# A hybrid decoder block on one core: the first norm without GpSimd, gates as the first columns, and block sums kept in PSUM for the convolutions

## The chip, the cores and the metric

One NeuronCore of a Trainium2 chip runs the whole program. The metric is device time in microseconds, the median of three runs of the program; beside it stands one execution that the hardware profiler recorded. PE is TensorE (matrix products and transposes), DVE VectorE, ACT ScalarE, POOL GpSimd, SP the engine that issues all DMAs from one queue.

## The reference, cut to what matters

`x` is 1024 tokens by 1024 channels, all float32.

```python
def rmsnorm(x, g):
    return x * lax.rsqrt(jnp.mean(x * x, -1, keepdims=True) + EPS) * g

h = rmsnorm(x, norm_mix)
proj = h @ w_in                      # 1024 x 1024 x 11808
z, xBC, dt_raw, qkv, gate_logits = jnp.split(proj, offs, axis=-1)
y_ssm = mamba2_branch(z, xBC, dt_raw, ...) @ w_ssm_out
    # xBC = silu(causal_depthwise_conv(xBC, conv_w, conv_b)), 4 taps
    # chunked state space scan over 128 tokens, times silu(z), group norm
q, k, v = rope(q), rope(k), v        # 12 heads of 128, three dilated windows
y_att = dilated_attention_branch(q, k, v) @ w_att_out
gates = sigmoid(gate_logits + b_gate)            # 2 x 1024 channels
x = x + (gates[0] * y_ssm + gates[1] * y_att) @ w_mix_out
h = rmsnorm(x, norm_ffn)
x = x + (silu(h @ w_ffn_gate) * (h @ w_ffn_up)) @ w_ffn_down
return rmsnorm(x, norm_final)
```

## The kernel before

**Numbers.** A float32 product is three passes of PE: every operand is split into a rounded high part and the rest (`hhi`, `hlo`; for weights a CAST on ACT and a subtraction on DVE or POOL), and `mm3` adds hi by hi, lo by hi and hi by lo in PSUM. `hhi` and `hlo` hold the normed tokens turned round: channel on the partitions, `[128, token half, depth tile k of 8, 512 tokens]`.

**Columns.** The input projection is 92 columns of 128 channels (and 32 channels of dt): 16 z, 16 x, 4 b, 4 c, 36 for q, k and v, 16 gates. An x, b or c column goes through `conv_silu` (an ACT pass with the bias, three DVE multiply-adds of 1023, 1022 and 1021 elements, one more DVE pass), a z column through an ACT Tanh and two DVE half passes, a gate column through one Tanh on ACT.

**Stages of the projection**, in order: (1) the *head*: the first norm, and two *first columns* that are computed by quarters of 256 tokens, as soon as two of the eight token tiles are ready (`first_quarter`); (2) the *bridge*: `N_BRIDGE` direct columns (48 products of 512 columns each), while the sums for the next stage are made; the dt columns; (3) the *flat* stage: 20 pairs of columns, each by block multiplication with seven products of 12 matmuls instead of eight (class `Seven`): products come in the order 1, 6, 5, 7, 2, 3, 4, each in one of four PSUM tiles `bank` of 512; `prep` makes the weights' sums on POOL and their parts on ACT and DVE; `chain` adds the products up on DVE; `T1` to `T4` are sums of token blocks (POOL first, then DVE). A *heavy* pair is two x columns, or a b and a c; a *light* one two z or two gates; they alternate; (4) the *direct* stage: q, k, v and the remaining gates as direct columns, with the scan and the attention beside them. Merge, FFN (Seven again) and the last norm follow.

**The head.** For each pair `q` of token tiles `stat_task` takes squares on ACT, multiplies the tiles by `norm_mix` (held as `nm`, one row copied to all partitions) on POOL, and finds the inverse root `rs` on DVE with 15 small operations of 128x2 (`rsqrt_steps`); `tile_task` scales the tile by `rs`, and `split_tokens` transposes it on PE into two banks, casts to `hhi` on ACT and subtracts to `hlo` on DVE.

**Order.** A planner (`Pace`) writes the program: tasks are generators that yield the buffers that they need, engines have costs in a small table, and the main line of PE calls `tick` or `due` between matmuls so that ready tasks write their instructions. Order on an engine is fixed by that; at run time only semaphores decide. Buffers come from stores: 31 slots `slab` of 1024, 6 slots `own`, two PSUM tiles `wide` of 1024, four `bank`; a slot is free again when its last reader is done. All records have one line, that of a helper.

## Time and profile before

| what | value |
|---|---|
| median of 3 runs | 2230.18 us (2226.22 to 2230.81) |
| the profiled execution | 2226.1 us, of it 2224.3 us span |
| PE busy, and its mean granted clock | 2154.4 us (97 %), 0.987 |
| DVE, ACT, POOL busy | 1545.7, 879.5, 690.9 us |
| DMA | 299.83 MB, 134 GB/s to and from HBM |

PE works nearly all of the span, so time can be read as PE's work plus the stretches in which it waits (69.9 us) or runs at a lower clock. The span is from the first to the last instruction.

### The profile page before, as it was taken

How to read it: one execution, taken by the hardware profiler on the slowest of the kernel's cores; microseconds unless marked ns; L12 is line 12 of the kernel's file. 1: busy time of each engine (PE TensorE's matmuls, PEld its weight loads, DVE VectorE, ACT ScalarE, POOL GpSimd, SP SyncE). 2: the span in 40 equal slices, each digit the busy share in tenths (PEclk: the TensorE clock that was granted, in tenths of full speed). 3: DMA queues.
4: the chain of work that ended last, by engine and by line, in shares of the span. 5: the costliest groups of instructions: out<-in, count | busy, mean ns of one | idle time of the engine just before them, and what ended most of it. 6: DMA issues, size and time to landing. Idle time of an engine off the chain costs nothing. (4 is left out here: it accounts for less than half of the span.)

```text
span 2224.3 us, 27832 instructions
## 1 busy us (share of the span) xinstructions
PE 2154.4 (97%) x10476; PEld 1781.7 (80%) x10476; DVE 1545.7 (69%) x2094; ACT 879.5 (40%) x1565; POOL 690.9 (31%) x420
## 2 busy tenths in 40 slices
PE   5999999999999999999999999999999999999996
PEld 4777888887888888888888887888778888888885
DVE  7979888876567776765434337644797777757787
ACT  3334444434554555454332224323333233324444
POOL 5233333321344444542103003002445444420102
PEclk8999999999999999999999999999999999999998
DMA  3433434336354555652128457463233333339332
GB/s 126 126 90 108 124 101 124 104 114 202 122 187 123 162 154 160 185 150 73 39 76 248 140 176 245 133 188 123 59 95 109 114 100 96 122 137 346 118 95 100
DMA packets 302587, 299.83 MB, mean 135 GB/s; under 512 B 20028, under 2 KB 246260, under 8 KB 302196
## 3 DMA queue, kind: packets, MB, share of 16 engines
q1 hardware_dynamic: 302452, 298.05, 42.9%
q8 instruction: 82, 1.34, 0.3%
q14 instruction: 53, 0.43, 0.1%
HBM read 225.00 MB, written 73.01 MB: 134 GB/s over the span
## 5 line engine op out<-in xcount | busy, mean ns | idle before, releaser
L165 POOL TENSOR_TENSOR xr<-xr,nfin 128x512 f32<-128x512 f32 x16 | 21.8, 1367 | 185.4 <-ACT jk L165 185.0
L165 POOL TENSOR_TENSOR slab__13_12098<-h2hi,h2lo 128x1024 f32<-128x1024 f32 x1 | 3.1, 3142 | 120.8 <-PE wide__35_11738 L165 120.8
L165 POOL TENSOR_TENSOR slab__11_10598<-slab__11_10598,last__2_10581 128x1024 f32<-128x1024 f32 x1 | 2.5, 2501 | 122.1 <-DMA slab__11_10598<-yt_d 122.1
L165 POOL TENSOR_TENSOR more__3_12094<-h2hi,h2lo 128x512 f32<-128x512 f32 x2 | 2.6, 1294 | 63.2 <-DVE h2lo L165 63.2
L165 POOL TENSOR_TENSOR slab__15_4124<-slab__15_4124,slab__14_4121 128x1024 f32<-128x1024 f32 x1 | 2.3, 2339 | 63.2 <-DVE wide__3_4015 L165 63.2
L165 ACT ACTIVATE jk<-xr 128x512 f32<-128x512 f32 x16 | 10.1, 632 | 16.4 <-DVE xr L165 12.7
L165 POOL TENSOR_TENSOR slab__21_7103<-slab__21_7103,slab__32_9422 128x1024 f32<-128x1024 f32 x1 | 2.4, 2388 | 43.1 <-DMA slab__32_9422<-fd 43.1
L165 POOL TENSOR_TENSOR slab__3_1145<-slab__3_1086 128x512 f32<-128x512 f32 x1 | 1.6, 1554 | 43.3 <-PE bank__6_1094 L165 43.3
L165 PE MATMUL bank__1_281<-ident,slab__1_151 128*128 128x128 f32 x4 | 1.1, 435 | 12.7 <-ACT slab__1_151 L165 12.7
L165 DVE TENSOR_TENSOR rs<-rs,rt 128x2 f32<-128x2 f32 (+2 forms) x30 | 12.4, 412 | 0.8
L165 PE MATMUL wide__4_4172<-hhi,slab__17_3976 128*128 128x512 f32 x16 | 7.9, 495 | 4.6 <-DVE slab__3_4170 L165 4.6
L165 POOL TENSOR_TENSOR slab__48_15496<-slab__23_15188,slab__80_15309 128x512 f32<-128x512 f32 x1 | 1.3, 1292 | 32.1 <-DVE slab__80_15309 L165 32.1
L165 PEld LDWEIGHTS bank__1_281<-ident,slab__1_151 128*128 128x128 f32 x4 | 0.7, 217 | 12.9 <-ACT slab__1_151 L165 12.9
L165 PE MATMUL wide__1_183<-hlo,slab__1_242 128*128 128x256 f32 x32 | 9.6, 299 | 1.1 <-DVE hlo L165 1.1
L165 POOL TENSOR_TENSOR slab__22_9025<-slab__22_9025,slab__14_4121 128x1024 f32<-128x1024 f32 x1 | 2.4, 2404 | 25.8 <-ACT slab__22_9025 L165 25.8
L165 PE MATMUL bank__3_479<-ident,slab__1_154 128*128 128x128 f32 x4 | 1.1, 428 | 9.5 <-DVE slab__1_154 L165 9.5
L165 DVE TENSOR_TENSOR rt<-rt,rv 128x2 f32<-128x2 f32 (+2 forms) x30 | 9.7, 324 | 0.7
L165 PE MATMUL wide__1_183<-hhi,slab__1_242 128*128 128x256 f32 x32 | 9.5, 295 | 0.7 <-ACT hhi L165 0.7
L165 ACT ACTIVATE xr<-xr,or 128x512 f32<-128x512 f32 x8 | 5.8, 719 | 10.6 <-DVE or L165 10.5
L165 DVE TENSOR_TENSOR slab__14_8742<-slab__14_8742,slab__33_9452 128x1024 f32<-128x1024 f32 x1 | 1.2, 1226 | 12.4 <-DMA slab__33_9452<-fd 12.4
L165 DVE TENSOR_SCALAR rv<-sq 128x2 f32<-128x2 f32 x4 | 2.4, 608 | 10.6 <-ACT slab__1_161 L165 10.6
L165 POOL TENSOR_TENSOR slab__10_8743<-slab__10_8743,slab__14_4121 128x1024 f32<-128x1024 f32 x1 | 2.4, 2406 | 22.7 <-ACT slab__10_8743 L165 22.7
(7605 smaller groups left out, 8377.5 us busy)
## 6 DMA issues: line engine op xcount, KB each, us to landing
xr<-x_d SPq DMA_DIRECT2D x8, 512.0 KB, 6.5
out<-xr SPq DMA_DIRECT2D x16, 256.0 KB, 2.1
b_d<-hhi SPq DMA_DIRECT2D x1, 1024.0 KB
b_d<-hlo SPq DMA_DIRECT2D x1, 1024.0 KB, 7.8
slab__1_150<-in_x SPq DMA_DIRECT2D x1, 512.0 KB
slab__1_151<-in_x SPq DMA_DIRECT2D x1, 512.0 KB, 5.1
slab__1_158<-in_norm_mix SPq DMA_DIRECT2D x1, 512.0 KB
slab__1_165<-in_w_in SPq DMA_DIRECT2D x1, 512.0 KB, 7.4
```

Of the source, the lines that this page charges most:

```text
L165: r = call(*args, **kw)
```

## The change

1. **First norm.** POOL no longer multiplies by `norm_mix`. Token tiles 0 to 3 are scaled by `rs` and `nm` in one DVE operation. Tiles 4 to 7 (`half_task`) are only scaled by their `rs`, transposed by depth tile `k` (four tiles into one bank), and `norm_mix`, now a column of `par` after the transposition, is applied as the scale of the copies out of PSUM: `hhi` (ACT), `hlo` (DVE), and a third copy on ACT that is T3 or T2 itself, so that `t_rest` has nothing left to add. The first columns' second token half follows by `k` (`first_half`, 512 tokens wide).
2. **Inverse root.** 12 small operations instead of 15; one root for tiles 4 to 7.
3. **Columns.** Gates 0 and 1 are the first columns instead of b and c of group 0; the bridge is gates 2 to 4 instead of four z; the flat stage has 12 heavy and 8 light pairs instead of 11 and 9, so heavy ones stand next to each other at four places; 11 gates instead of 10 are direct columns.
4. **Flat sums.** The last additions of a pair are written to two `wide` PSUM tiles (for the last pair to `own`), and convolutions, z and gates read them there.
5. **dt.** The chain of dt waits until flat pair 6 and yields between its operations.
6. **From flat to direct.** Before, the first k and the first q column both had their first token half done ahead of the reload of `hhi` and `hlo` (event `b12`); now only k, and q follows whole.
7. `mm3` calls `pace.wait`, which changes the planner's clock and no instruction.

```diff
-N_BRIDGE = 4
-N_FLAT_GATES = 6
+N_BRIDGE = 3
+N_FLAT_GATES = 0
...
         for _ in range(3):
-            nc.vector.tensor_tensor(t, r, r, ALU.mult)
+            nc.vector.scalar_tensor_tensor(t, r, -0.5, r, ALU.mult, ALU.mult)
             yield [t]
             nc.vector.tensor_tensor(t, t, v, ALU.mult)
             yield [t]
-            nc.vector.tensor_scalar(t, t, -0.5, 1.5, ALU.mult, ALU.add)
-            yield [t]
-            nc.vector.tensor_tensor(r, r, t, ALU.mult)
+            nc.vector.scalar_tensor_tensor(r, t, 1.5, r, ALU.add, ALU.mult)
...
+            o = yield from outs()
+            yield from arrive(7, (o["22"], c12), (c21, c21))
             for p, c, name in ((2, c11, "11"), (3, c12, "12"), (4, c21, "21")):
-                yield from arrive(p, (c, c))
+                yield from arrive(p, (o[name], c))
...
-    first = [plan_a(XBC0 + DI)[0], plan_a(XBC0 + DI + 512)[0]]
+    first = [plan_a(GATE0 + i * P)[0] for i in range(2)]
...
-    bridge = [direct("z", 0, f) for f in range(N_BRIDGE)]
+    bridge = [direct("gate", 2 + i) for i in range(N_BRIDGE)]
...
     def stat_task(q):
...
-            if q or i:
-                yield [nm]
-                nc.gpsimd.tensor_tensor(xt.v, xt.v, nm.v, ALU.mult)
...
     def tile_task(i):
...
+        nc.vector.scalar_tensor_tensor(xt.v, xt.v, rs, nm.v, ALU.mult, ALU.mult)
         yield [xt]
-        if i == 0:
-            nc.vector.scalar_tensor_tensor(xt.v, xt.v, rs, nm.v, ALU.mult, ALU.mult)
-        elif i == 1:
-            nc.scalar.activation(xt.v, xt.v, AF.Copy, scale=rs)
-        else:
-            nc.vector.tensor_scalar(xt.v, xt.v, rs, None, ALU.mult)
...
+    def half_task():
+
+        yield "rs2"
+        for i in range(4):
+            xt, rs = xts[4 + i].v, rscale[2][:, i:i + 1]
+            if i % 2:
+                nc.vector.tensor_scalar(xt, xt, rs, None, ALU.mult)
+            else:
+                nc.scalar.activation(xt, xt, AF.Copy, scale=rs)
...
+        for k in range(KD):
+            yield from bank.room()
+            pt = bank.get([P, 512])
+            for i in range(4):
+                tp(pt.v[:, i * P:(i + 1) * P], xts[4 + i].v[:, k * P:(k + 1) * P], ident)
+            hv = hhi[:, 1, k, :]
+            yield [pt]
+            nc.scalar.activation(hv, pt.v, AF.Copy, scale=nm_t(k))
+            nc.vector.scalar_tensor_tensor(hlo[:, 1, k, :], pt.v, nm_t(k), hv.bitcast(F32), ALU.mult, ALU.subtract)
+            nc.scalar.activation(A.T[("T3", "T2")[k // 4]][k % 4 // 2].v[:, k % 2, :], pt.v, AF.Copy, scale=nm_t(k))
+            pt.free()
+            pace.fire(f"hk{k}")
...
+    def first_half():
+        ws = [w_get(first[u]) for u in range(2)]
+        for k in range(KD):
+            pace.until(f"hk{k}")
+            for u, (hi, lo) in enumerate(ws):
+                mm3(fps[u].v[:, 512:], hi[:, k, :], lo[:, k, :], hhi[:, 1, k, :], hlo[:, 1, k, :], k == 0, k == KD - 1)
+                tick()
...
+        def outs():
+            place = own if i == len(flat) - 1 else wide
+            yield from place.room(2)
+            res.extend(place.get([P, S]) for _ in range(2))
...
     for i in range(len(flat)):
+        if i == 6:
+            pace.fire("spare")
...
-    ps = [u(ths=(0,)) for u in units[:2]]
+    ps = units[0](ths=(0,))
     pace.until("b12")
-    for u, t in zip(units[:2], ps):
-        u(t, (1,))
-    units = units[2:]
+    units.pop(0)(ps, (1,))
```

POOL in the head, before, from its first work on; `slab__1_150` to `157` are the token tiles, `158` is `nm`, `165` and `242` the first weight tile and its high part, `670` to `675` the sums for T1 and T4 of token half 0.

```order
L165 TENSOR_TENSOR slab__1_151<-slab__1_151,slab__1_158 128x1024
L165 TENSOR_TENSOR slab__1_243<-slab__1_165,slab__1_242 128x1024
L165 TENSOR_TENSOR slab__1_152<-slab__1_152,slab__1_158 128x1024
L165 TENSOR_TENSOR slab__1_153<-slab__1_153,slab__1_158 128x1024
L165 TENSOR_TENSOR slab__1_154<-slab__1_154,slab__1_158 128x1024
L165 TENSOR_TENSOR slab__1_155<-slab__1_155,slab__1_158 128x1024
L165 TENSOR_TENSOR slab__1_156<-slab__1_156,slab__1_158 128x1024
L165 TENSOR_TENSOR slab__1_157<-slab__1_157,slab__1_158 128x1024
L165 TENSOR_TENSOR slab__1_670<-hhi,hlo 128x1024
L165 TENSOR_TENSOR slab__1_671<-hhi,hlo 128x1024
L165 TENSOR_TENSOR slab__1_674<-hhi,hlo 128x1024
L165 TENSOR_TENSOR slab__1_675<-hhi,hlo 128x1024
```

POOL in the head now, again from its first work on; the last rows are the first flat pair's weight sums.

```order
L166 TENSOR_TENSOR slab__1_596<-hhi,hlo 128x1024
L166 TENSOR_TENSOR slab__1_597<-hhi,hlo 128x1024
L166 TENSOR_TENSOR slab__1_600<-hhi,hlo 128x1024
L166 TENSOR_TENSOR slab__1_601<-hhi,hlo 128x1024
L166 TENSOR_TENSOR slab__2_620<-slab__2_618 128x512
```

The four sums are now POOL's first work; they wait for the two `hlo` operations of token tile 3 and for nothing later.

ACT in the head before, in the second token half: one CAST for each of the banks into which tiles 4 to 7 are transposed.

```order
L165 CAST hhi<-bank__3_479 128x4x128
L165 CAST hhi<-bank__3_486 128x4x128
L165 CAST hhi<-bank__4_491 128x4x128
L165 CAST hhi<-bank__4_501 128x4x128
L165 CAST hhi<-bank__4_547 128x4x128
```

ACT in the head now, where the second token half is scaled and copied out (tiles 4 and 6 are `slab__1_154` and `156`, the banks one depth tile each, `slab__1_447` a part of T3).

```order
L166 ACTIVATE slab__1_154<-slab__1_154,rs_11_269 128x1024
L166 ACTIVATE slab__1_156<-slab__1_156,rs_11_269 128x1024
L166 ACTIVATE hhi<-bank__3_459,par 128x512
L166 ACTIVATE slab__1_447<-bank__3_459,par 128x512
L166 ACTIVATE hhi<-bank__3_467,par 128x512
L166 ACTIVATE slab__1_447<-bank__3_467,par 128x512
L166 ACTIVATE hhi<-bank__4_475,par 128x512
```

Now each bank has two copies on ACT with the `hlo` operation of DVE between them: the second copy waits for that operation, and the bank is free after it.

DVE in the flat stage before, the middle of one heavy pair (`own__2_1063` and `1064` are the pair's two columns, `own__3_1248` and `1268` what `conv_silu` accumulates, banks are products).

```order
L165 TENSOR_TENSOR own__2_1064<-bank__11_1222,own__2_1064 128x512
L165 SCALAR_TENSOR_TENSOR own__3_1248<-own__2_1063,par,own__3_1248 128x1023
L165 SCALAR_TENSOR_TENSOR own__3_1248<-own__2_1063,par,own__3_1248 128x1022
L165 SCALAR_TENSOR_TENSOR own__3_1248<-own__2_1063,par,own__3_1248 128x1021
L165 TENSOR_TENSOR slab__3_1231<-slab__4_1217,slab__3_1231 128x512
L165 SCALAR_TENSOR_TENSOR own__3_1268<-own__2_1064,par,own__3_1268 128x1023
```

DVE in the flat stage now, the same place of a heavy pair that follows another one.

```order
L166 TENSOR_TENSOR wide__6_1443<-bank__12_1447,own__3_1339 128x512
L166 TENSOR_TENSOR wide__6_1444<-bank__12_1468,own__4_1340 128x512
L166 SCALAR_TENSOR_TENSOR own__4_1494<-wide__6_1443,par,own__4_1494 128x1023
L166 SCALAR_TENSOR_TENSOR own__4_1494<-wide__6_1443,par,own__4_1494 128x1022
L166 SCALAR_TENSOR_TENSOR own__4_1494<-wide__6_1443,par,own__4_1494 128x1021
L166 SCALAR_TENSOR_TENSOR own__5_1499<-wide__6_1444,par,own__5_1499 128x1023
L166 SCALAR_TENSOR_TENSOR own__5_1499<-wide__6_1444,par,own__5_1499 128x1022
```

The sum and its reader have moved from `own` (SBUF) to `wide` (PSUM); the next pair's seventh product, the first that is written to a `wide` tile, waits until these readers are done.

SP at the end of the flat stage, before (`in_rope` is the table for q and k, `xq_d` the store of a finished x column).

```order
L165 DMA xq_d_120<-own__17_4034 512x1x256
L165 DMA xq_d_120<-own__13_4045 512x1x256
L165 DMA slab__20_4117<-in_w_in 128x8x128
L165 DMA slab__16_4119<-in_rope 128x1024
L165 DMA slab__14_4121<-in_rope 128x1024
```

SP at the end of the flat stage now (`zq_d` is the store of a finished z column).

```order
L166 DMA zq_d_124<-own__16_3943 512x1x256
L166 DMA zq_d_124<-own__17_3960 512x1x256
L166 DMA slab__17_4008<-in_w_in 128x8x128
L166 DMA slab__3_4010<-in_rope 128x1024
L166 DMA slab__3_4012<-in_rope 128x1024
```

The table's loads stand behind the last pair's stores as before, but the last pair is now a light one.

## Rows read from the trace of the kernel before

**Rows 1.** The page's head and part 1 (engine, busy us, share, instructions).

```profile
span 2224.3 us, 27832 instructions
...
PE 2154.4 (97%) x10476; PEld 1781.7 (80%) x10476; DVE 1545.7 (69%) x2094; ACT 879.5 (40%) x1565; POOL 690.9 (31%) x420
```

**Rows 2.** Waits of PE: us in total, times, longest.

```profile
PE bank__1_281 L165 <- ACT slab__1_151 L165: 12.7, 1, 12.7
PE bank__3_479 L165 <- DVE slab__1_154 L165: 9.5, 1, 9.5
PE wide__4_4172 L165 <- DVE slab__3_4170 L165: 4.6, 1, 4.6
```

**Rows 3.** Timeline of the head, POOL: start us, us, operation, [idle before <-releaser].

```profile
40.80 2.39 POOL L165 TENSOR_TENSOR slab__1_670<-hhi,hlo 128x1024 f32<-128x1024 f32 x1
```

**Rows 4.** Timeline of the head, DVE, at the same time.

```profile
38.54 2.32 DVE L165 TENSOR_TENSOR rt<-rt,rv 128x2 f32<-128x2 f32 x1
...
40.90 2.32 DVE L165 TENSOR_SCALAR rt<-rt 128x2 f32<-128x2 f32 x1
```

**Rows 5.** Timeline of the head, DVE, early.

```profile
8.21 0.17 DVE L165 TENSOR_SCALAR rt<-rv 128x2 int32<-128x2 int32 x1
...
20.80 1.28 DVE L165 SCALAR_TENSOR_TENSOR slab__1_150<-slab__1_150,rs,slab__1_158 128x1024 f32<-128x1024 f32 x1
```

**Rows 6.** Timeline of the head, ACT.

```profile
6.82 1.06 ACT L165 ACTIVATE slab__1_161<-slab__1_151 128x1024 f32<-128x1024 f32 x1
...
20.86 1.15 ACT L165 ACTIVATE slab__1_151<-slab__1_151,rs 128x1024 f32<-128x1024 f32 x1 [5.40 <-DVE rt L165]
23.22 0.59 ACT L165 CAST hhi<-bank__1_281 128x512 fp32r<-128x512 f32 x1 [1.21 <-PE bank__1_281 L165]
...
74.36 1.21 ACT L165 ACTIVATE own__1_662<-wide__1_184,par 128x1024 f32<-128x1024 f32 x1 [1.67 <-PE wide__1_184 L165]
```

**Rows 7.** Windows of the flat stage: us, engines' busy us (instructions), PEclk, DMA.

```profile
130.00:150.00 20.00, 17.84 (x77) 13.89 (x75) 19.36 (x19) 12.17 (x19) 8.18 (x4) 1.00 0.25 72
150.00:190.00 40.00, 35.39 (x138) 28.00 (x139) 36.70 (x43) 15.21 (x24) 19.39 (x10) 0.91 0.33 96
190.00:250.00 60.00, 60.00 (x267) 49.69 (x266) 55.63 (x65) 24.70 (x37) 23.34 (x15) 1.00 0.33 97
```

**Rows 8.** Windows of the passage to the direct stage, columns as before.

```profile
547.50:552.10 4.60, 0.01 (x1) 0.05 (x1) 2.56 (x4) 3.06 (x3) 4.49 (x2) 0.83 1.03 407
552.10:560.00 7.90, 7.90 (x27) 6.25 (x27) 3.96 (x5) 3.54 (x10) 2.14 (x2) 0.67 0.95 294
```

**Rows 9.** Timeline there, SP (time to issue) and DVE.

```profile
538.19 0.51 SPq L165 DMA_DIRECT2D xq_d<-own__13_4045  x1
...
539.49 1.33 SPq L165 DMA_DIRECT2D slab__16_4119<-in_rope  x1
...
546.31 1.23 DVE L165 TENSOR_TENSOR wide__3_4015<-wide__3_4015,slab__16_4119 128x1024 f32<-128x1024 f32 x1 [8.15 <-DMA slab__16_4119<-in_rope]
```

**Rows 10.** Timeline of the head, PE.

```profile
22.06 1.12 PE L165 MATMUL bank__1_281<-ident,slab__1_151 128*128 128x128 f32 x4 [12.70 <-ACT slab__1_151 L165]
```

**Rows 11.** Timeline of the first heavy flat pair, DVE.

```profile
155.43 0.68 DVE L165 TENSOR_TENSOR own__2_1064<-bank__11_1222,own__2_1064 128x512 f32<-128x512 f32 x1
156.03 6.18 DVE L165 SCALAR_TENSOR_TENSOR own__3_1248<-own__2_1063,par,own__3_1248 128x1023 f32<-128x1023 f32 x3
...
162.74 3.91 DVE L165 SCALAR_TENSOR_TENSOR own__3_1268<-own__2_1064,par,own__3_1268 128x1023 f32<-128x1023 f32 x3
...
173.73 2.28 DVE L165 SCALAR_TENSOR_TENSOR own__3_1268<-own__2_1064,own__3_1268 128x1024 f32<-128x1024 f32 x1
```

**Rows 12.** Timeline, DVE with a PSUM operand, and POOL.

```profile
80.69 3.91 DVE L165 SCALAR_TENSOR_TENSOR own__1_662<-wide__1_184,par,own__1_662 128x1023 f32<-128x1023 f32 x3
...
86.01 1.21 DVE L165 SCALAR_TENSOR_TENSOR own__1_629<-wide__1_183,own__1_629 128x1024 f32<-128x1024 f32 x1
...
85.08 2.17 POOL L165 TENSOR_TENSOR slab__2_697<-slab__2_697,slab__2_693 128x512 f32<-128x512 f32 x1
```

More of the change, by code (lines that the diff above doesn't have):

```diff
@@ L297, in due, with wait @@
             self._step(min(ready, key=lambda k: (k[1], k[0], k[2])))
+    def wait(self, out, ins):
+        while True:
+            at = max([self.wr.get(_key(a), (0.0, ""))[0] for a in ins] + [self.rd.get(_key(out), (0.0, ""))[0]])
+            if at <= self.t:
+                return
+            nxt = max(self.t, min([at] + [k[0] for k in self.tasks]))
+            self.stall += nxt - self.t
+            self.t = nxt
+            self.due()
+            if nxt == at:
+                return
     def until(self, ev):
@@ L640, in prep, with chain @@
                 u.free()
-        def chain(self, i, c11, c12, c21, c22, then):
+        def chain(self, i, c11, c12, c21, then, outs):
             add = ALU.add
@@ L965, in dt_task @@
         pace.fire("dtm")
+        yield "spare"
         yield [dtT]
@@ L1265, in gate_task @@
     def gate_task(i, ps):
-        if ps.owner is own:
-            t = ps
-        else:
-            yield from slabs.room()
-            t = slabs.get([P, S])
+        dst = own if i < 2 + N_BRIDGE + N_FLAT_GATES else slabs
+        yield from dst.room()
+        t = dst.get([P, S])
         yield [ps]
-        nc.scalar.activation(t.v, ps.v, AF.Tanh, bias=bg_half[:, i:i + 1], scale=0.5)
-        if t is not ps:
-            ps.free()
+        for a in range(0, S, 512):
+            nc.scalar.activation(t.v[:, a:a + 512], ps.cut(a, a + 512), AF.Tanh, bias=bg_half[:, i:i + 1], scale=0.5)
+        ps.free()
         yield [t]
@@ L1456, in hybrid_block @@
     w_done(first[1])
-    pace.spawn(c_task(0, fps[1]), 0.3, -1)
     pace.spawn(dt_task())
-    flat_cols = [[column(*c) for c in pair] for pair in flat]
-    A = Seven("in", hhi, hlo, [[cols_of(w_in, 0, KD, col, P) for col, _ in pair] for pair in flat_cols],
-              lambda th, j: f"h{th * 4 + j}")
     def save_b12():
@@ L1844, in second, with outs @@
             cd.free()
[L1846 removed]
+        def outs():
+            yield []
+            return {"11": c11, "12": c12, "21": c21, "22": c22}
+        yield from F.chain(f - N_DIRECT, c11, c12, c21, {"11": lambda: gated(0, c11), "12": second}, outs)
         nc.vector.tensor_tensor(a.v[:, 0], a.v[:, 0], c21, ALU.mult)
```

139 lines of the change are left out of this document (81 added, 58 removed).

## The prediction

> **What bounds the kernel now.** The page's head and part 1 come first: PE is busy 2154.4 of 2224.3 us [rows 1]. The change leaves PE's work as it is: 92 columns before and after, 20 pairs by block multiplication in both, two first columns and 50 direct ones in both. So the time can only move by PE's waits, 69.9 us in all, and by stretches in which PE runs at its lower clock. The list of PE's waits says where the 69.9 are: 12.7 and 9.5 us in the head, each for a token tile that had not been scaled yet, and 4.6 in the passage from the flat to the direct stage, for rope [rows 2]. The others are smaller.
>
> The timeline says why the head waits. POOL works through operations of 2.3 to 2.4 us one behind the other [rows 3], and in that time DVE's operations of 128x2, each link of one chain, last 2.32 us [rows 4], where the same kind takes 0.17 us with POOL idle [rows 5]: the inverse root advances by one small operation for each operation of POOL. The first high part of tokens is cast at 23.22 and the second first column goes to its convolution at 74.36 [rows 6], so the head ends at about 74.2.
>
> The windows of the flat stage's start have PE 17.84 of 20 and 35.39 of 40 us busy, with DVE at 19.36 and 36.70, and a granted clock of 0.91 in the second; from 190 on PE is full at 1.00 [rows 7]. So DVE, loaded with the dt chain, token sums and convolutions, makes PE wait 2.2 + 4.6 = 6.8 us there, and the clock costs 35.4 x 0.09 = 3.2 more. The passage shows the same pattern: 4.6 us with PE idle, then 7.9 us at 0.67, of which 0.33 x 7.9 = 2.6 are lost [rows 8]. What is late there is a table: its load is issued at 539.49, right behind the stores of the last heavy pair (538.19) that hold the queue, and DVE waits 8.15 us for it [rows 9].
>
> **The change, the head.** I followed the new order with durations from rows. Until 8.0 all is as before. The root is 12 links of 0.2 us (0.17 [rows 5] and the step to the next) with no POOL work near it: done at 10.4. Two scalings of 1.28 [rows 5] end at 12.9. ACT then has, in order, two squares of 1.06 (and 0.2 for the read of the sum), a weight cast of as many elements put at 1.05, four casts of 0.59 [rows 6]; they end at 17.0, DVE's four `hlo` near 18.1, and the first columns start at about 17.5. The second root runs 19.3 to 21.7 behind the second weight's subtraction, which is now DVE's; two scalings to 24.2; transposes (four in 1.1 us at the low clock [rows 10]), casts and `hlo` to 28.05, with the last four squares between them on ACT, done at 28.45.
>
> The third root, for tiles 4 to 7, starts there, and meets the one thing left on POOL in the head: the four sums for T1 and T4 wait only for `hlo` of token tile 3, so they start at about 26.4 and run 4 x 2.33 = 9.3 us, until 35.7. As in [rows 3, 4] the chain passes one link per sum; the eight or so that are left then take 1.6 us: root done at 37.4, against 30.9 if nothing held it. I take the held value, since the operands are of the same kind, and keep 6.5 us as the price in the other direction. Two scalings of 1.15 on ACT [rows 6] lead to 39.7 (DVE's two and the copy of `par` lie beside them); PE has run out at about 32.8 and waits some 7 us.
>
> Then eight depth tiles. ACT's copy to `hhi` (0.65, a little over a plain cast's 0.59), DVE's `hlo` (0.70, a bank operation is 0.68 [rows 11]), ACT's copy to T: the third waits for the second in the program, and ACT's next `hhi` stands behind it, so a period is 2.0 to 2.05 us with their hand-overs. First transposes to 40.7, seven periods 14.4, a last 1.35, one weight cast of 1.05 between, six matmuls of 60 / 267 = 0.225 us [rows 7]: 58.8. PE's own work per tile is six matmuls and four transposes, 1.8 us at full clock, so it keeps up there; at half clock it is 3.6, and 8 x 3.6 = 28.8 would be the bound: end at 69.5. After the 4.6 us of the passage the clock was low for less than 8 us [rows 8]; so I expect it low for two tiles, 3 us late, of which the later tiles get back 0.25 each: 1 us is left, and the head ends at 59.8. **Gain 74.2 - 59.8 = 14.4**, between 4.7 (low clock throughout) and 21.9 (nothing held, full clock).
>
> The Trainium skill, "PSUM — Partial Sum Buffer", in "PSUM bank collisions raise a hardware error", has it that two engines must not be on the same bank at once even to read. That is why the third copy can't run beside DVE's `hlo`. No row here shows two readers of a bank side by side; were it allowed, the period would be PE's 1.8 at full clock and the head would end some 2 us earlier.
>
> **The flat stage.** Work on a heavy pair's DVE side is 7 additions and 7 weight subtractions at 0.6 us step to step, and two convolutions of 3.91 + 1.21 ([rows 11], and from PSUM alike [rows 12]): 18.6 us; PE needs 84 x 0.225 = 18.9 for a pair. A light pair needs 14 x 0.6 + 4 x 0.6 = 10.8. So two heavy ones in a row just fit and the light one after them gives 8 us back. A convolution that reads SBUF beside POOL took 6.18 and its last pass 2.28 [rows 11]; a last pass that read PSUM took 1.21 in the middle of a POOL operation [rows 12], so the move to `wide` takes the longest DVE operations out of POOL's reach. At the start the gates leave DVE nothing to do (ACT only), the dt chain (some 5 us of DVE) waits until pair 6 and then spreads through the 4.4 us that DVE has free in 60 [rows 7], and T2 and T3 come finished from the head. **Gain 6.8 + 3.2 = 10.0**, between nothing and that.
>
> **The passage.** The last pair is now a light one: its stores wait for four half passes (2.4 us) where two convolutions (10.2 us) stood ahead of them, so the table lands some 8 us earlier, more than the 4.6 that PE waited; the whole q column (48 x 0.225 = 10.8 us) stands as cover where before half a one did. **Gain 4.6 + 2.6 = 7.2**; if the load is still late, nothing.
>
> **The rest.** Three small operations fewer in other roots, at most 0.5 us. Eleven rather than ten late gates and one first bridge column fewer are the same PE work. The tail and the small waits after 1300 may move by 3 us either way, since nothing there is changed; I put them at 0. Tiles 6 and 7 are loaded behind five small loads, one of them new; they are first read at about 26, some 19 us after tile 1 had arrived for its square [rows 6], so this costs nothing unless those loads take over 15 us.
>
> Sum: 14.4 + 10.0 + 7.2 = 31.6; 2226.1 - 31.6 = 2194.5 for an execution like the profiled one, whose span of 2224.3 has 1.8 around it. The three timed runs have a median of 2230.18, 4 above it: 2198.6. I say 2196, between the two.
>
> **Rivals.**
> (B) The head gains less: the clock stays low or the hand-overs are longer, and a depth tile costs 2.8 to 3.6 instead of 2.05: 6 to 10 us lost, about 2204. For it: the wait ahead of the tiles is longer than that of [rows 8]. Against it: in the tiles PE is nearly always busy. Chance 0.12.
> (C) Heavy pairs in a row fall behind: POOL's four sums per pair hold weight subtractions, up to 1.7 each; at 2.8 us a pair (DVE's 55.6 of 60 less what the operations need alone, 46.6, over 3.2 pairs) two heavy ones need 42.8 for 37.8, which uses up the 5 us of slack worked out under (D). Where it runs over, four places at 2.5 to 5 us take 10 to 20 back: 2206 to 2216. Chance 0.12.
> (E) POOL's sums don't hold the third root, because DVE's link comes first or the sums slip: 6.5 more, 2189. Against it [rows 3, 4]. Chance 0.08.
> (D) Slower: the seventh product's sum waits until both `wide` tiles are read. Alone, the readers take about 14 us from the pair's last sum; the next pair's seventh product is its fourth and its bank is filled again seven products later than the pair's start, 18.9 us after that sum, so 5 us are to spare. Before, the first heavy pair's readers took from 155.4 to 176.0, 20.6 us [rows 11]. If POOL holds convolutions in PSUM as it held those in SBUF, 24 us are needed, 5 too many, at 12 heavy pairs: 60 us, 2254. It ends on the slow side from 3 us a pair. The undisturbed pass in [rows 12] speaks against it. Chance 0.06.
>
> **The numbers.** The forecast (2184 to 2205, with the unknown costs above) has 0.60, E 0.08, B and C 0.12 each, D 0.06, and 0.02 for no change. A measurement can tell about 0.2 %, 4.5 us, from nothing: the first four and the upper C are all more than that faster: faster 0.90, same 0.03, slower 0.07. From 2184 to 2213 holds the forecast, E, B and most of C.
>
> **What would show it.** In the changed profile: DVE's small operations of 128x2 at 0.17 for two roots, and 2.3 for four links of the third beside POOL; a PE wait of 6 to 8 us for the scaled tiles; eight copies of T on ACT about 2.05 apart; the head's end near 60; no PE wait above 1 us between there and the passage, clock 1.00; no wait for rope. Wrong would be waits on `bank` tiles for a `wide` reader, a granted clock near 0.5 through the depth tiles, or the sums on POOL somewhere else.

## The result, and the profile after

The changed kernel takes 2199.64 us (median of 4 runs, 2198.87 to 2202.68) where the kernel before takes 2229.69 (median of 4, 2226.22 to 2230.81): a ratio of 0.987, 95 % interval 0.9853 to 0.9887. The forecast was 2196, its range 2184 to 2213. The profiled execution took 2199.41 us, against 2194.5 worked out for one like it.

The page's head and part 1 of the changed kernel, as in [rows 1]:

```profile
span 2197.6 us, 27736 instructions
...
PE 2146.8 (98%) x10428; PEld 1770.6 (81%) x10428; DVE 1502.6 (68%) x2050; ACT 885.9 (40%) x1590; POOL 631.5 (29%) x406
```

The span is 26.7 us shorter. PE waits 2197.6 - 2146.8 = 50.8 us where it waited 69.9, which is 19.1 of it; the other 7.6 are busy time that PE no longer spends. The clock accounts for about all of that: its mean rose from 0.987 to 0.994, and by the two traces PE was busy for 27.1 us at the lower of its two levels before and for 10.8 now; half of such time is lost, 13.6 and 5.4 us.

Waits of PE in the changed kernel (in total, times, longest), to be held against [rows 2]:

```profile
PE bank__3_459 L166 <- ACT slab__1_154 L166: 6.0, 1, 6.0
PE bank__123_12515 L166 <- DVE slab__30_12422 L166: 3.7, 1, 3.7
PE bank__121_10666 L166 <- DVE more__4_10718 L166: 3.0, 1, 3.0
...
PE bank__1_253 L166 <- DVE slab__1_150 L166: 2.6, 1, 2.6
...
PE bank__23_2264 L166 <- DVE own__7_2108 L166: 1.6, 1, 1.6
```

The waits of 12.7 and 9.5 us for scaled tokens have become 2.6 and 6.0, and that of 4.6 for rope is gone. The second and third row are in the FFN's part of the program, which the change doesn't touch.

Where the time came from is seen by cutting the span at the same matmul in both traces. Times are starts on PE, from the timelines. Bridge and flat stage are taken together, because the dt columns' small products stood in the bridge before and stand in the flat stage now; one column of 10.9 us went from the bridge to the direct stage, and is put back in the last column.

| matmul | before | after | gained since the one above |
|---|---|---|---|
| last of the head | 74.0 | 59.8 | 14.3 |
| first of the direct stage | 525.6 | 491.9 | 33.7 - 14.3 - 10.9 = 8.5 |
| first of the merge | 1244.4 | 1216.2 | 28.2 - 33.7 + 10.9 = 5.4 |
| first of the down projection | 2026.9 | 2000.6 | -1.9 |
| end of the span | 2224.3 | 2197.6 | 0.4 |

The parts of the gain are known less well than to 0.1 us, since each is read from one execution of either kernel. The third root, of 128x4, starts at 28.74 here; in the other runs with that root in this document it starts anywhere from 27.2 to 30.4, and in four that have the same instructions up to the head's end, at the same matmul step, the head ends at 59.9 to 61.2. So below, a time in the head is also counted from that root.

The head's middle, changed kernel, from the timeline (start us, us, operation, idle before it and releaser): DVE, then POOL, then ACT.

```profile
28.74 0.86 DVE L166 TENSOR_SCALAR rv<-sq 128x4 f32<-128x4 f32 x1 [0.35 <-ACT slab__1_161 L166]
29.63 2.32 DVE L166 TENSOR_SCALAR rt<-rv 128x4 int32<-128x4 int32 x1
31.98 2.29 DVE L166 TENSOR_SCALAR rs<-rt 128x4 int32<-128x4 int32 x1
34.30 2.25 DVE L166 SCALAR_TENSOR_TENSOR rt<-rs 128x4 f32<-128x4 f32 x1
36.59 0.16 DVE L166 TENSOR_TENSOR rt<-rt,rv 128x4 f32<-128x4 f32 x1
...
27.16 2.41 POOL L166 TENSOR_TENSOR slab__1_596<-hhi,hlo 128x1024 f32<-128x1024 f32 x1 [26.72 <-DVE hlo L166]
...
34.19 2.34 POOL L166 TENSOR_TENSOR slab__1_601<-hhi,hlo 128x1024 f32<-128x1024 f32 x1
...
38.16 1.15 ACT L166 ACTIVATE slab__1_154<-slab__1_154,rs 128x1024 f32<-128x1024 f32 x1 [9.46 <-DVE rs L166]
...
42.63 0.69 ACT L166 ACTIVATE slab__1_447<-bank__3_459,par 128x512 f32<-128x512 f32 x1 [0.82 <-DVE hlo L166]
...
44.72 0.69 ACT L166 ACTIVATE slab__1_447<-bank__3_467,par 128x512 f32<-128x512 f32 x1 [0.82 <-DVE hlo L166]
...
58.72 0.69 ACT L166 ACTIVATE slab__1_450<-bank__5_536,par 128x512 f32<-128x512 f32 x1 [0.82 <-DVE hlo L166]
```

The first four links of the root end within 0.05 us of POOL's four sums, the last at 36.55; from then a link takes 0.16 and the next starts 0.2 later. ACT waits 9.46 us for the root. From the root's start to the head's end it is 31.0 us. The eight copies of T are 2.08 apart, each behind 0.82 of waiting for DVE's `hlo`, but for one gap of 3.58 with a weight cast in it.

Windows of the changed kernel from the bridge on (columns as in [rows 7]):

```profile
100.00:260.00 160.00, 160.00 (x717) 132.46 (x717) 141.87 (x178) 69.20 (x109) 50.76 (x35) 1.00 0.37 109
260.00:300.00 40.00, 37.23 (x164) 29.80 (x163) 39.01 (x48) 15.60 (x25) 11.54 (x8) 1.00 0.32 96
300.00:490.00 190.00, 190.00 (x850) 157.13 (x849) 160.43 (x198) 78.57 (x117) 44.36 (x32) 1.00 0.41 125
490.00:600.00 110.00, 109.92 (x639) 89.45 (x639) 68.74 (x94) 57.84 (x119) 47.01 (x31) 1.00 0.61 193
900.00:1000.00 100.00, 98.86 (x529) 82.58 (x527) 58.95 (x77) 42.07 (x82) 28.32 (x14) 1.00 0.31 88
...
1650.00:2000.00 350.00, 350.00 (x1545) 289.57 (x1544) 245.77 (x320) 107.59 (x184) 140.45 (x96) 1.00 0.38 126
```

The flat stage's start, which had a clock of 0.91 and 6.8 us of waits in [rows 7], is full at 1.00, and so is the passage (0.67 in [rows 8]). There is one new place: from 260 to 300 PE waits 2.8 us while DVE is busy 39.01 of 40. There the delayed dt chain meets two heavy pairs in a row. (The last row is for a comparison further on.)

No pass of a convolution in the flat stage takes more than 1.29 us now, so that three in a row never take more than 3.92; before, nine such rows took 4.8 to 6.8, one of them in [rows 11]. The last passes, which read their sum from PSUM, take 1.21 to 1.23, where one from SBUF took 2.28 [rows 11]. The Trainium skill, "SBUF — State Buffer", in "Who interferes with whom", has it that a DVE instruction with two inputs in SBUF contends with a GpSimd one that reads SBUF; by these two numbers the trace agrees.

### The profile page after: what moved, and what is told of

It reads as the page before. It is cut to its first block, busy times and chain, and to the rows that moved or that the text cites. A ratio compares the mean times of both kernels' runs of the same rounds, so it can differ in the third digit from the quotient of the medians.

```text
span 2197.6 us, 27736 instructions
## 1 busy us (share of the span) xinstructions
PE 2146.8 (98%) x10428; PEld 1770.6 (81%) x10428; DVE 1502.6 (68%) x2050; ACT 885.9 (40%) x1590; POOL 631.5 (29%) x406
## 3 DMA queue, kind: packets, MB, share of 16 engines
q1 hardware_dynamic: 302468, 298.06, 43.5%
## 5 line engine op out<-in xcount | busy, mean ns | idle before, releaser
L166 POOL TENSOR_TENSOR slab__2_4015<-slab__2_4015,slab__3_4012 128x1024 f32<-128x1024 f32 x1 | 2.4, 2397 | 59.8 <-DMA slab__3_4012<-in_rope 59.8
L166 ACT ACTIVATE jk<-xr 128x512 f32<-128x512 f32 x16 | 10.1, 632 | 15.4 <-DVE xr L166 11.2
L166 PE MATMUL wide__1_184<-hhi,slab__1_248 128*128 128x256 f32 (+1 forms) x24 | 8.8, 367 | 2.6 <-ACT hhi L166 2.6
L166 PE MATMUL wide__1_184<-hlo,slab__1_248 128*128 128x256 f32 (+1 forms) x24 | 8.9, 371 | 2.3 <-DVE hlo L166 2.3
L166 POOL TENSOR_TENSOR slab__1_596<-hhi,hlo 128x1024 f32<-128x1024 f32 x1 | 2.4, 2406 | 26.7 <-DVE hlo L166 26.7
L166 PE MATMUL bank__1_186<-ident 128*128 128x128 f32 x36 | 5.9, 343 | 2.7 <-DMA ident<-in_consts 2.7
L166 PEld LDWEIGHTS wide__1_184<-hhi,slab__1_248 128*128 128x128 f32 x24 | 5.3, 219 | 3.9 <-ACT hhi L166 3.7
L166 PEld LDWEIGHTS wide__1_184<-hlo,slab__1_248 128*128 128x128 f32 x24 | 5.3, 219 | 3.9 <-DVE hlo L166 3.8
```

What stands on the lines that cost most here:

```text
L166: r = call(*args, **kw)
```

## The experiments

Theory of the prediction: the head's end is set by the third root, held by POOL's sums, and then by eight periods on ACT and DVE; the flat sums in PSUM and the earlier table give the rest. Rivals: the root isn't what sets it; removing POOL's multiplications alone gives the gain; the light last pair or the whole q column each suffices.

### Release the third root

One small operation on POOL ahead of the four sums reads the root's result, so that the sums start after it.

```diff
             yield self.tile_ready(0, 3)
+            if self.tag == "in":
+                yield "par"
+                g = small("gp", 4)
+                nc.gpsimd.tensor_tensor(g, rscale[2], rscale[2], ALU.add)
```

> The changed kernel, with one small GpSimd operation of 128x4 ahead of the four sums for T1 and T4 that reads the root of token tiles 4 to 7, so that the sums start when that root is done instead of beside it. Theory (POOL's operations hold the chain of the third root): the root ends at about 31.0 instead of 38.1, 7 us earlier, but the two scalings on DVE right behind it are the next to meet the sums. If those are held too, one by the first sum and one by the second, DVE is done near 36 and the head ends 3 to 4 us earlier, about 56; if a scaling with one operand from SBUF is not held, the whole 6 to 7 us is kept, about 53. Rival (the chain of 128x4 operations is slow for another reason, such as the squares that end just before it): the small operations stay near 2.3 us and nothing moves.

2224.22 us (2221.53 to 2225.14, 8 runs), ratio 0.9977 (0.9967 to 0.9988): nearly all of the gain is lost. From the timeline of this run, POOL and DVE:

```profile
29.79 2.81 POOL L166 TENSOR_TENSOR slab__1_598<-hhi,hlo 128x1024 f32<-128x1024 f32 x1
...
29.39 0.16 DVE L166 SCALAR_TENSOR_TENSOR rs<-rt,rs 128x4 f32<-128x4 f32 x1
...
30.30 2.85 DVE L166 TENSOR_SCALAR slab__1_157<-slab__1_157,rs 128x1024 f32<-128x1024 f32 x1
33.07 4.61 DVE L166 COPY dcol<-hrow 64x16 f32<-64x16 f32 x2
...
38.07 2.04 DVE L166 TENSOR_SCALAR par<-par 128x120 f32<-128x120 f32 x2
```

The root itself is free: 2.35 us from start to end, no link above 0.17. But the sums then held what came next: the scaling of tile 7 (2.85, where it takes 0.75), two small copies into `dcol` (4.61, where they take 0.35) and the scaling of `par` behind them; `par` holds the column that the first depth tile needs. The head ended at 57.9, only 1.9 earlier, and most of that is the root's earlier start (27.20): from there to the head's end it is 30.7 us, against 31.0. That doesn't explain a loss of 25 us: from the head to the first direct matmul this run needs 438.4 us, where the changed kernel needs 432.1, and the later stages run behind too. Two things are mixed, and the next runs take them apart.

The same operation, but reading `par`, so that the sums start behind the scalings and the copies too:

```diff
...
+                yield "par"
+                g = small("gp", 4)
+                nc.gpsimd.tensor_tensor(g, par[:, 136:140], par[:, 136:140], ALU.add)
```

> As the run before, but the small GpSimd operation reads the column of gate biases in par, which DVE writes after the two scalings: the four sums then run beside the depth tiles, in which DVE reads a PSUM bank and one SBUF tile. Theory: root done near 31.0, scalings near 33.5, head's end 6 to 7 us earlier than the changed kernel's, near 53, whole run near 2193; DVE's eight hlo operations stay at 0.75 us although POOL is busy beside four of them. Rival: hlo operations are held like the root, 2.3 us each for four tiles, and most of the gain is gone (head near 58).

2216.19 us (2214.22 to 2216.86), 0.9942 (0.9925 to 0.9958). The head ended at 52.5, 7.3 earlier (from the root's start 23.8 us, against 31.0), and the end still came 17 us later. The root and the scalings weren't held. So the loss lies behind the head and isn't the sums' place.

What both runs share is a new tile. The next run writes the operation's result into four unused columns of `par` instead, so that every address stays:

```diff
...
+                nc.gpsimd.real.tensor_tensor(par[:, 176:180], par[:, 136:140], par[:, 136:140], ALU.add)
```

> As the second of the two runs with later sums, but the small GpSimd operation writes to unused columns of par, so no tile is added, and the order on every engine is that of the changed kernel. Theory (the head gains 7.3 us, and what was lost after it came with the added tile of 16 bytes, which moved the tiles behind it): head's end near 52.5, 512-wide matmuls at 0.2265 us step to step everywhere, 2192 to 2194 for the run. Rival (what the head gives is taken back in the flat stage, where DVE is full): head near 52.5 but the first direct column starts no earlier than 490, 2198 to 2200.

2194.27 us (2188.80 to 2198.04), 0.9841 (0.9818 to 0.9863). The instructions stand on every engine as in the changed kernel, with that one more on POOL. Timeline, DVE and POOL:

```profile
29.87 0.17 DVE L166 TENSOR_SCALAR rv<-sq 128x4 f32<-128x4 f32 x1 [0.36 <-ACT slab__1_161 L166]
...
32.07 0.16 DVE L166 SCALAR_TENSOR_TENSOR rs<-rt,rs 128x4 f32<-128x4 f32 x1
...
32.94 0.75 DVE L166 TENSOR_SCALAR slab__1_157<-slab__1_157,rs 128x1024 f32<-128x1024 f32 x1
...
35.40 2.35 POOL L166 TENSOR_TENSOR slab__1_597<-hhi,hlo 128x1024 f32<-128x1024 f32 x1
...
35.80 0.75 DVE L166 SCALAR_TENSOR_TENSOR hlo<-bank__3_459,par,hhi 128x512 fp32r<-128x512 f32 x1 [0.64 <-ACT hhi L166]
```

The head ends at 53.7, 6.1 earlier than in the changed kernel, although the root starts 1.1 later here; from the root's start it is 23.9 us, against 31.0. So the sums' price, which the prediction put at 6.5, is 7.2. The first direct matmul comes 4.8 earlier and the span ends 7.8 earlier; the medians are 5.4 apart, and the intervals of the two ratios still touch (up to 0.9863 here, from 0.9853 there). The sums now lie beside the `hlo` operations, which read PSUM and one SBUF tensor, and these keep their 0.75.

And the tile alone, which no instruction uses:

```diff
+    small("gp", 4)
     cst_b, hrow_t = slabs.get([P, C_W - P]), ...
```

> The changed kernel with one more tile of 128x4 floats that nothing reads or writes, ahead of the big tiles in SBUF: addresses move, no instruction does. Theory (the place of the operands in SBUF sets the step of the 512-wide matmuls): the head ends at 59.8 as in the changed kernel, but a part of the matmuls takes 0.24 instead of 0.2265 us and the run is 14 to 18 us slower, 2214 to 2218. Rival (those runs were slower for the later sums themselves): 2199 to 2201.

2224.55 us (2218.79 to 2228.30, 10 runs), 0.9979 (0.9968 to 0.999). No instruction stands elsewhere on any engine, and the run takes 25 us more than the changed kernel, more than the 14 to 18 that were looked for. The matmuls on one tile of the FFN, in the changed kernel and then in this run (duration min/median/max in ns, first and last start):

```profile
L166 PE MATMUL bank__144_13963<-h2hi,slab__62_13726 x8: 389/389/389, 1777.4 to 1779.9; 128*128 128x512 f32 x8
```

```profile
L166 PE MATMUL bank__144_13964<-h2hi,slab__62_13727 x8: 392/395/398, 1798.4 to 1801.0; 128*128 128x512 f32 x8
```

A window of this run of 350 us in which PE waits for nothing (the changed kernel's is the last row of its windows above):

```profile
1650.00:2000.00 350.00, 350.00 (x1520) 285.04 (x1519) 247.24 (x319) 105.41 (x179) 149.41 (x104) 1.00 0.34 111
```

The same matmul takes 395 instead of 389 ns, and PE does 1520 instead of 1545 of them in 350 us, at the same clock and with no wait: 1.6 %. The first two runs of this section do 1520 in the same window as well, the third 1545. So in the first two the new tile, not the order, cost the time. The kernel before does 1546 in the same window, so the change itself has neither gained nor lost in this way.

### The period of a depth tile

The third copy of a tile (T) is issued behind the next tile's `hhi`:

```diff
...
             nc.scalar.activation(hv, pt.v, AF.Copy, scale=nm_t(k))
+            if late:
+                late.pop()()
             nc.vector.scalar_tensor_tensor(hlo[:, 1, k, :], pt.v, nm_t(k), ...)
-            nc.scalar.activation(A.T[...]..., pt.v, AF.Copy, scale=nm_t(k))
-            pt.free()
+            late.append(lambda k=k, pt=pt: t_copy(k, pt))
...
```

> The changed kernel with ACT's third copy of each depth tile issued one tile later, behind the next tile's copy to hhi, so that it no longer stands between DVE's hlo and the next hhi. Theory (the period of 2.08 us is the chain of three operations on two engines): ACT needs 2 x 0.6, DVE 0.75 and PE 1.8 us at full clock per tile, so the period falls to about 1.8 and the head ends 1.5 to 2 us earlier; PE's low clock at the start may eat part of it. Rival (the banks or the two readers of one bank set the period): it stays at 2.08, no gain.

2201.48 us (2199.04 to 2201.85), 0.9875 (0.986 to 0.989): no difference from the changed kernel. The copies come 0.9 to 2.1 apart, but the head ends only 1.2 earlier. A part of that is the root's start, which was 1.7 later in this run: from there to the head's end it is 28.2 us, against 31.0, so the edit gives 2.8. The start, from the timeline:

```profile
30.43 0.85 DVE L166 TENSOR_SCALAR rv<-sq 128x4 f32<-128x4 f32 x1 [0.36 <-ACT slab__1_161 L166]
```

A window in the depth tiles says why it isn't more:

```profile
41.00:46.00 5.00, 4.60 (x19) 4.01 (x20) 3.02 (x9) 4.06 (x6) 0.00 (x0) 0.50 0.01 2
```

The clock is at 0.50, the lower of its two levels (1.2 of 2.4 GHz), behind a wait of 6.04 us, and PE is the bound there. The direct stage's first matmul is at 492.1 against 491.9: from the head's end to there this run needs 433.5 us and the changed kernel 432.1, and a run below that has the changed kernel's instructions up to the passage (the first under "The passage") needs 434.1. So a gain of this size can't be told at that place.

### Nothing but GpSimd's multiplications

In the kernel before, POOL's multiplications by `norm_mix` go, and DVE scales every tile by `rs` and `nm` in one operation; all else stays.

```diff
-            if q or i:
-                yield [nm]
-                nc.gpsimd.tensor_tensor(xt.v, xt.v, nm.v, ALU.mult)
...
-        if i == 0: ...
-        else:
-            nc.vector.tensor_scalar(xt.v, xt.v, rs, None, ALU.mult)
+        yield [nm]
+        nc.vector.scalar_tensor_tensor(xt.v, xt.v, rs, nm.v, ALU.mult, ALU.mult)
```

> The kernel before with one thing changed: GpSimd doesn't multiply by norm_mix, DVE scales all eight token tiles by root and norm_mix in one operation, by token tiles as before. It tells how much of the head's 14.3 us is GpSimd alone. By a walk with the same durations: first root 2.5 us earlier, third and fourth root beside the four sums for T1 and T4 only, so one of them is held for 9 us instead of both being behind POOL for 14; the head ends at about 62 to 66 instead of 74: 8 to 12 us faster than the kernel before. Rival (the depth tiles are what does it): under 4 us.

2231.02 us (2222.74 to 2233.68, 10 runs), 1.0002 (0.9991 to 1.0013): the 8 to 12 us looked for didn't come; the head ends at 73.0, 1.0 earlier. Timeline, POOL and DVE:

```profile
42.41 2.38 POOL L165 TENSOR_TENSOR slab__1_667<-hhi,hlo 128x1024 f32<-128x1024 f32 x1 [0.70 <-DVE rs L165]
...
42.44 2.37 DVE L165 TENSOR_TENSOR rt<-rs 128x2 f32<-128x2 f32 x1
44.84 2.30 DVE L165 TENSOR_TENSOR rt<-rt,rv 128x2 f32<-128x2 f32 x1
...
56.34 1.22 DVE L165 TENSOR_TENSOR rt<-rs 128x2 f32<-128x2 f32 x1
```

The sums for T1 and T4 take the place that the multiplications had, and later those for T2 and T3, of 1.3 each, hold the last root. So the head's gain needs the other halves of part 1 and 2: one root for tiles 4 to 7, and T2 and T3 finished by ACT, which leave only four sums for POOL. How much each of these gives wasn't tried; nor was part 3 undone by itself, so what the gates as first columns give to the head and the bridge is open.

### The flat stage

The old place of dt (part 5 undone):

```diff
-        yield "spare"
...
-        yield 4.0
...
```

> The changed kernel without its fifth part: the dt chain starts as soon as its matmuls are done, in the bridge, with no pauses between its operations. Theory A (the new PE waits of 2.8 us between 260 and 300 come from the dt chain in a stretch with two heavy pairs in a row): they vanish, and since DVE has 12 us free in the bridge between 80 and 100, nothing takes their place: 2 to 3 us faster than the changed kernel. Theory B (the delay was needed: the chain pushes T4 and the first weights late, as in the kernel before, where PE waited 6.8 us and lost 3.2 more to the clock): 3 to 10 us slower. Theory C (heavy pairs in a row alone make the waits): they stay and the time is the same.

2201.99 us (2198.12 to 2204.98), 0.9878 (0.9863 to 0.9894), no difference. Two of its windows:

```profile
100.00:200.00 100.00, 97.71 (x431) 79.76 (x430) 88.50 (x106) 46.53 (x73) 33.73 (x24) 1.00 0.33 98
...
250.00:300.00 50.00, 50.00 (x226) 41.33 (x225) 45.81 (x55) 21.66 (x32) 13.83 (x10) 1.00 0.29 85
```

The 2.8 us of waits at 260 to 300 are gone, so the dt chain is what makes them; in their place stand 2.3 at 100 to 200. Another 1.7 at 400 to 490 are in the last pair, where a run with the dt chain in its new place also waits 1.8 (the row with `own__15_3778` under "The passage"), so they can't be put down to dt. DVE's work is the same, and the waits go where it is put.

The sums back in SBUF (part 4 undone): the two columns of a pair are added up in `own`, and convolutions, z and gates read them there.

```diff
+        ca, cb = own.get([P, S]), own.get([P, S])
...
-            place = own if i == len(flat) - 1 else wide
-            yield from place.room(2)
-            res.extend(place.get([P, S]) for _ in range(2))
...
+            return {"11": ca.cut(0, 512), "12": ca.cut(512, S), "21": cb.cut(0, 512), "22": cb.cut(512, S)}
```

> The changed kernel without its fourth part: a pair's last sums go to own, in SBUF, as before, and convolutions and z read them there; the order of pairs with heavy ones in a row stays. Theory (PSUM operands keep the convolutions out of POOL's reach): a convolution's three operations take up to 6.2 instead of 3.9 us where POOL works beside them, 2 to 5 us more per heavy pair, which the four places with two heavy pairs in a row can't hide: PE waits of 8 to 25 us in the flat stage. Rival (the place doesn't matter, the spare DVE time of light pairs is enough): under 3 us more.

2218.65 us (2213.71 to 2222.02 in three runs; a fourth of 6713.01, of which there is no trace, is out of the ratio), 0.9944 (0.9924 to 0.9965). The first direct matmul comes at 509.9, 18.0 later. From 100 to 490 PE is idle 15.2 us instead of 2.8, and over 150 us of this its clock is 0.97. Its longest wait, PE, and what DVE and POOL do ahead of it:

```profile
308.99 0.80 PE L166 MATMUL bank__25_2384<-hhi,slab__9_2152 128*128 128x512 f32 x1 [7.01 <-DVE own__6_2237 L166]
...
301.59 2.28 DVE L166 SCALAR_TENSOR_TENSOR own__7_2280<-own__7_2092,own__7_2280 128x1024 f32<-128x1024 f32 x1
303.79 1.74 DVE L166 TENSOR_TENSOR slab__8_2340<-slab__8_2272,slab__8_2340 128x512 fp32r<-128x512 f32 x1
305.46 2.28 DVE L166 SCALAR_TENSOR_TENSOR own__11_2290<-own__6_2093,own__11_2290 128x1024 f32<-128x1024 f32 x1
...
302.75 2.24 POOL L166 TENSOR_TENSOR slab__5_2351<-slab__8_2272,slab__10_2274 128x512 f32<-128x512 f32 x1
```

The last passes of two convolutions, both inputs in SBUF, take 2.28 beside POOL's sums; the addition that frees PE's bank stands behind them. In the changed kernel the same two passes take 1.21 each. The 18 us are more than the 8.5 that the change gains in the bridge and the flat stage: without the move to PSUM, its other parts lose time there. At the end of the span 14.3 of the 18 are left.

### The passage

Part 6 undone, k and q both with their first half ahead of the reload:

```diff
-    ps = units[0](ths=(0,))
+    ps = [u(ths=(0,)) for u in units[:2]]
     pace.until("b12")
-    units.pop(0)(ps, (1,))
+    for u, t in zip(units[:2], ps):
+        u(t, (1,))
+    units = units[2:]
```

> The changed kernel with the passage of before: the first token half of both k and q, then the second of both. Theory (the table for rope is early because the last flat pair is light): no PE wait of more than 1 us at the passage, the time stays within 1 us. Rival (the whole q column was the cover): the wait of 4 to 5 us of before comes back, with 2 us of low clock.

2213.17 us (2204.84 to 2215.21), 0.992 (0.9899 to 0.9941). Two of PE's waits, from the list, and a row of DVE:

```profile
PE bank__46_4113 L166 <- ACT slab__17_4119 L166: 4.5, 1, 4.5
...
PE bank__44_3861 L166 <- DVE own__15_3778 L166: 1.8, 1, 1.8
```

```profile
513.87 1.23 DVE L166 TENSOR_TENSOR wide__22_3931<-wide__22_3931,slab__11_4030 128x1024 f32<-128x1024 f32 x1 [14.27 <-ACT slab__14_4035 L166]
```

With the light last pair kept, the stall comes back, so that pair isn't what removes it. With the halves interleaved, k is complete at 511.8 instead of 502.5, and as the direct stage starts at 495.3 instead of 491.9 in this run, 5.9 of that is the edit's; its rope on DVE starts at 513.87 instead of 505.03, ACT's work for rope and scan bunches behind it, and PE has 4.5 us with nothing to do, not for the table but for ACT. The direct stage takes 732.1 us instead of 724.3, 7.8 more; the other 5.5 of the 13.3 us by which the span is longer lie before and behind it, 3.4 of them ahead of anything that the edit moves.

The last two pairs exchanged, so that a heavy one is last, with part 6 kept:

```diff
+    flat[-2:] = flat[:-3:-1]
     flat_cols = [[column(*c) for c in pair] for pair in flat]
```

> The changed kernel with the last two flat pairs exchanged: a heavy pair is last. Theory (the light last pair lets the table out earlier): the table's load leaves some 8 us later and the first rope with it; with the whole q column as cover PE may still be late by 0 to 5 us at the passage. It also takes one place with two heavy pairs in a row away. If the time stays within 1 us, the q column alone is cover enough; if 4 to 7 us come back, the light pair was what removed the wait.

2198.34 us (2197.53 to 2200.64), 0.9862 (0.9848 to 0.9877): no slower than the changed kernel. Its list of waits has one at this place:

```profile
PE wide__23_4068 L166 <- DVE slab__15_4062 L166: 1.5, 1, 1.5
```

### The old root

```diff
-            nc.vector.scalar_tensor_tensor(t, r, -0.5, r, ALU.mult, ALU.mult)
+            nc.vector.tensor_tensor(t, r, r, ALU.mult)
...
+            nc.vector.tensor_scalar(t, t, -0.5, 1.5, ALU.mult, ALU.add)
...
```

> The changed kernel with the inverse root of before, 15 small operations instead of 12. Theory: 3 x 0.2 us later for each of the first two roots, of which the second stands behind other work, and 0.6 for the third behind the sums: the head ends 0.6 to 1.2 us later, the run stays within 0.2 % of the changed kernel. Rival (an operation with one operand, which the old root has, passes POOL's operations where the fused ones are held): the third root ends earlier and the head with it, by up to 2 us.

2214.83 us (2209.14 to 2214.97), 0.9935 (0.9918 to 0.9951), where no difference above 0.2 % was looked for. The head ends 1.8 later, more than the 0.6 to 1.2 looked for: the third root takes 11.2 us instead of 9.4. Nothing more is lost up to the first direct matmul (493.8), but the direct stage takes 9.2 us more. The wait that makes most of it, from the list, and the window around it, to be held against the changed kernel's:

```profile
PE bank__107_7844 L166 <- DVE half__19_7728 L166: 4.2, 1, 4.2
```

```profile
900.00:1000.00 100.00, 95.19 (x502) 79.94 (x501) 59.97 (x81) 45.36 (x87) 35.96 (x20) 0.97 0.35 102
```

The root's operations are in the planner's sums too: with three more of them in each root, some 200 of DVE's 1940 other instructions stand in another order, up to far into the direct stage, and one such place makes PE wait 4.2 us for DVE. The matmul step isn't the cause: PE does 1545 matmuls from 1650 to 2000, as in the changed kernel. That these 9 us come from the order is read from the two orders and this wait; it wasn't tried by itself.

### What could go together

The sums behind the scalings (in unused columns of `par`), T late, and the heavy pair last, each as in its own run:

```diff
...
+                nc.gpsimd.real.tensor_tensor(par[:, 176:180], par[:, 136:140], par[:, 136:140], ALU.add)
...
+            late.append(lambda k=k, pt=pt: t_copy(k, pt))
...
+    flat[-2:] = flat[:-3:-1]
```

> The changed kernel with three edits together: the four sums after the scalings (no tile added), ACT's third copy one tile later, and the last two flat pairs exchanged. If they add up: 7.3 us from the root and 1.2 from the copies in the head, 1.3 from the exchange, 2189 to 2191. If the flat stage's full DVE takes back what the head gives: 2196 to 2199.

2188.46 us (2186.69 to 2191.88), 0.9818 (0.9802 to 0.9834): faster than both kernels, than the changed one by (0.987 - 0.9818) x 2228 = 11.6 us, and a little below the 2189 to 2191 of the three gains added up. The head ends at 49.9, 19.5 us from the root's start at 30.41. The window in its depth tiles:

```profile
33.00:40.00 7.00, 6.98 (x50) 5.67 (x49) 4.68 (x11) 6.14 (x10) 4.23 (x3) 1.00 0.00 1
```

Without the wait of 6 us ahead of the tiles the clock is 1.00 and PE is full, so that the shorter period, which alone gave 2.8 us, now gives 23.86 - 19.54 = 4.3, both counted from the root's start.

## Why the prediction was right, point by point

**What bounds it.** PE's waits and its low clock were the only two things that the change could move, and they hold all 26.7 us of the span: 19.1 and 7.6.

**The head: 14.4 said, 14.3 measured.** That the two agree to 0.1 us is luck, since the head's end differs by 1.4 us between runs of the same instructions. But the steps hold one by one. The first columns start at 15.8 (17.5 said), the sums start at 27.16 (26.4 said) and end at 36.5 (35.7); the root is done at 38.1 (37.4), PE waits 6.0 us (6 to 8); the period is 2.08 (2.0 to 2.05); the clock is low for the first tiles only, transposes taking 0.42 us until 43.5 and 0.27 from 44.0. The root was held for three full links and a part of a fourth (four said). From the first transposition to the head's end it is 20.4 us, against 19.7 in the run without the wait: the low clock cost at most 0.7, where 1 was said. The runs with the sums elsewhere show the cause, not only the place: without the hold the head is 7.2 us shorter from the root's start, where the prediction's price was 6.5 (rival E's). That rival didn't occur.

**The flat stage: 10.0 said, 8.5 measured** with the bridge. What was named is gone, both the 6.8 us of waits and the low clock. The term was too large because the dt chain, put at no cost since DVE had 4.4 us free in 60, fell on two heavy pairs in a row and cost 2.8 there. The place is one of rival C's four, and 2.8 is at the lower end of its 2.5 to 5 us, but the cause isn't C's: with dt moved away the same two pairs run without a wait, and the other three places show none either. So C didn't occur. The step that failed here is the dt chain's cost of nothing: 4.4 us free in 60 is a mean over heavy and light pairs, and two heavy ones leave 2 x (18.9 - 18.6) = 0.6. "No wait above 1 us between the head and the passage" was wrong for this place (1.6). Undoing the move of dt gained nothing, for the same work then stands in PE's way earlier.

**The passage: 7.2 said, 5.4 measured** to the end of the direct stage. The 4.6 us and the low clock are gone. 1.1 us of new waits stand at 900 to 1000. Of the two reasons given, the earlier table behind a light pair and the whole q column as cover, the runs leave the second: with a heavy last pair 1.5 us of wait appear and the time stays, and with two halves the stall returns although the pair is light. What the prediction hadn't seen is that with halves k is complete 5.9 us later in the stage, and with it rope and the scan's first step on ACT.

**The rest: 0 said, -1.5 measured**, within the 3 us allowed. The sum is 14.3 + 8.5 + 5.4 - 1.5 = 26.7 against 31.6; in medians it is 30.1, because the profiled execution of before lay 3.5 us below its median and that of after at it.

**Rivals B and D** didn't occur: the tiles cost 2.08 each, and PE has no wait for a `wide` tile in the flat stage. D's 24 us don't follow from its rows, which give 20.6 us, or 22.9 if both convolutions had been held as one was; its places would have cost less. No rival of the prediction was about tile sizes: a small tile can move the time by 25 us through addresses alone, and `par` grew by 32 columns in this change. Here the count of matmuls in a full window stayed as before, which the diff could not tell.

## What to carry to other kernels

Ask of work that is taken from an engine what moves up into its place: removing POOL's multiplications alone gave nothing, since its next operations held the same chain on DVE, and the sums that held it came to cost nothing only where they stood beside work with an operand in PSUM. Before a run is read as the cost of an edit, look at the matmul step of a window in which PE waits for nothing; if it differs though no instruction has moved, look at addresses; scratch space that was already there kept them here. Count a stage from its own start: an edit worth 2.8 us looked like 1.2, because the root had started later in that run. A stall can be paid again in the clock behind it: shortening a period was worth 2.8 us behind a stall of 6 us, and 4.3 without that stall.

## What the runs showed of the hardware that wasn't expected

A tile of four floats per partition that no instruction uses made the same 128x512 matmul take 395 instead of 389 ns, at a granted clock of 1.00, and the run 25 us longer. Which operand's address does it wasn't tried.

DVE operations with only one tensor as input are held beside POOL's sums as well: a scaling of 128x1024 took 2.85 instead of 0.75 us, two copies of 64x16 4.61 instead of 0.35. One with an input in PSUM beside one in SBUF kept its 0.75.
